# A gated-attention block on one core: the first pair placed later, one operation moved to ScalarE, GpSimd's transfers in parts

## The chip, the core and the metric

The kernel runs on one NeuronCore of a Trainium2 chip. Five engines work beside each other, each with its own queue in order: TensorE (PE: matrix products; its weight loads are listed as PEld), VectorE (DVE), ScalarE (ACT), GpSimd (POOL) and SyncE (SP, which here issues most loads). Sixteen DMA engines move data. The metric is the device time of one execution, in microseconds (us). Less is better.

## The reference

One decoder block over 256 tokens of width 2048, in float32. After a root-mean-square norm, one projection w_in gives q, k, v, an output gate, a low-rank decay, three streams for a short convolution and two merge gates:

```python
gk = einsum('bsr,rk->bsk', gk_low, w_gk_up) + b_gk_up
log_g = log_sigmoid(gk) / 16
# chunks of 64 tokens, 4 heads; bcum = cumsum(log_g) within a chunk
q_dec, k_dec = q * dk**-0.5 * exp(bcum), k * exp(-bcum)
o = tril(q_dec @ k_dec.T) @ v + q_dec @ state      # state carried from chunk to chunk
y_a = rmsnorm(o, gla_norm_w) * silu(g_out)
y_b = gate_b * (u[t-2]*w[0] + u[t-1]*w[1] + u[t]*w[2])   # u = gate_c * xc
h = x + (sigmoid(merge_a) * y_a + sigmoid(merge_b) * y_b) @ w_out
h = h + (silu(rmsnorm(h) @ w_gate) * (rmsnorm(h) @ w_up)) @ w_down
out = rmsnorm(h)
```

The hidden width is 5632. Nearly all the arithmetic lies in the products with w_in, w_out, w_gate_up and w_down.

## The kernel before

**Precision.** Each fp32 product is made of three products of a 32-bit format with fewer bits: every operand is split into a high part (`hi`) and a rest (`lo`), and `mm3` (L358) adds hi·lo, lo·hi and hi·hi. So each weight piece of 128 x 1024 is loaded by SyncE (`raw`), cast by ScalarE (`high`, L246 to 249) and subtracted by VectorE (`low`, L251 to 254) before TensorE can use it.

**Pieces.** A group of 512 output columns comes in eight pieces ("eights", `eights`, L398): 12 matmuls of 512 columns for a piece. Some groups go in pairs (`PAIRS_IN`, L76) by a scheme with seven block products in place of eight (`sevens`, L423): 28 pieces of 6 matmuls, where 16 of the pieces are sums of weight blocks that VectorE adds first (`sum_of`, L256; L272 and L277). A sevens piece gives TensorE half the work of an eights piece and VectorE more. So eights pieces are dealt in between the sevens pieces: `DEAL` (L81) says after each of a pair's 28 pieces how many eights pieces follow, and `PLACE` (L77) how many stand ahead of the pair. The order in w_in is: k0 and q0 in eights (16 pieces), the eights pieces of v0 by `PLACE`, then the pairs k2 with q2, v2 with v3, gc0 with xc0 and so on, each with its eights in between. Then come the w_out groups and the hidden layer, which are dealt in the same way.

**Order.** All is issued in one program order. When a piece is taken (`take`, L348), the piece five places later is fetched and cast, and the one four places later is subtracted. The buffers (six raw, six hi, five lo) tie how far each engine can run ahead. After each piece a counter, the tick, goes up by one (L330), and work hung on that tick is issued: `later(n, f)` and `at(tick, f)`. The framework may move an instruction within its engine's queue, save where `pin` keeps it in program order. The constants at the end of the file (L1306 on) give the ticks.

**The decay tables**, ticks 11 to 27. `x_rstd` (L669) gives the norm's factor; `spread_rstd` (L675) turns it into a row by a matmul, `split_low` (L719) splits the low-rank part, and `decay_logits` (L727) makes the logits z in PSUM and reads them twice: ScalarE takes |z|, VectorE min(z, 0). ScalarE then does a sigmoid and a logarithm of the whole tile, VectorE adds (`log_decay`, L750), sums along each chunk with eight scans (`sum_decay`, L754), and makes differences (`tables_within`, L776). ScalarE takes exponentials. `tables_across` (L787) has four operations on GpSimd and three exponentials on ScalarE. `decayed` (L707) transposes k and q and multiplies them by the tables; `scores` and `attend` follow.

**Convolution.** `conv` (L970) takes u of a gc pair, copies it to u1 and u2 shifted by one and two tokens with GpSimd's DMAs (`move`, L974), and multiplies and adds in five pinned steps on VectorE (`step`, L981). The taps are loaded by GpSimd (`load_taps`, L966). `merge` (L995) joins the branches. In the w_out stage `read_h` (L1120) loads the residual x in four parts, the first from SyncE's queue, the others from GpSimd's.

Of the kernel before, what the change touches and what calls it, by code (L numbers as in the profile page):

```python
# [43 lines left out]
def plan():  # L44
# [32 lines left out]
PLACE = (4, 0, 4, 0, 0, 0, 0)  # L77
# [4 lines left out]
    "k2": "00100 10010 01110 01010 00101000",  # L82
    "v2": "10100 11110 01200 00210 10000100",
    "gc0": "10011 00201 21111 22121 00210001",
    "gc1": "01110 11111 01002 00210 00010001",
    "gc2": "10110 12211 11202 11110 01000111",
    "gc3": "01111 01121 01001 11201 00111010",
    "g3": "30100 00100 00210 01201 00000000",
# [102 lines left out]
def block_kernel(ctx, tc, x, xt, cols_in, gkw_in, gku_in, gnw, conv_w, finw, w_in, w_out, w_gu, w_dn, out):  # L191
# [54 lines left out]
    def high(raw, piece, a=0, b=None):  # L246
        hi, n = piece[0], piece[2]
        ks = slice(a, b or n)
        nc.scalar.copy(hi[:, ks, :], raw[:, ks, :])  # L249
# [377 lines left out]
    eps = const.tile([P, 1], F32, name="eps")  # L627
    mask = gpool.tile([P, NT, P], I8, name="mask")
# [46 lines left out]
    def spread_rstd():  # L675

        rb_ps = aux([P, T], "rb_ps")
        for t in range(NT):
            spread = gpool.tile([P, P], F32, tag="sch", name="spread", bufs=2)
            nc.vector.tensor_scalar(out=spread, in0=ones, scalar1=r1[:, t:t + 1], scalar2=None, op0=ALU.mult)  # L680
            nc.tensor.matmul(rb_ps[:, t * P:(t + 1) * P], lhsT=spread, rhs=ident, start=True, stop=True)
        nc.vector.tensor_copy(rb, rb_ps)
# [14 lines left out]
    later(12, spread_rstd)  # L697
# [29 lines left out]
    def decay_logits(m0):  # L727
# [7 lines left out]
        for j in range(2):  # L735
            m = m0 + j
            nc.scalar.activation(za[:, m, :], zp[:, j, :], AF.Abs, bias=bgk[:, m:m + 1])
            nc.vector.tensor_scalar(out=zm[:, m, :], in0=zp[:, j, :], scalar1=bgk[:, m:m + 1], scalar2=0.0,
                                    op0=ALU.add, op1=ALU.min)
# [10 lines left out]
    def log_decay():  # L750
        nc.scalar.activation(za, za, AF.Ln)
        nc.vector.tensor_tensor(out=zm, in0=zm, in1=za, op=ALU.add)
# [50 lines left out]
    at(13, split_low)  # L803
    for i in range(4):
        at(14 + i // 2, lambda i=i: decay_logits(2 * i))
    at(17, lambda: nc.scalar.activation(za, za, AF.Sigmoid))
    at(19, log_decay)
    at(20, lambda: sum_decay(0))
    at(21, lambda: sum_decay(4))
    at(22, tables_within)  # L810
    at(23, lambda: exponential(eq, inv))
    at(25, tables_across)
# [132 lines left out]
    for n, (what, t) in enumerate((("k", 0), ("k", 1), ("q", 0), ("q", 1))):  # L945
        at(DECAY_AT + n, lambda what=what, t=t: decayed(what, 0, t, rows[f"{what}0"][:, t, :]))
# [19 lines left out]
    def load_taps(i):  # L966
        taps[i] = ew.tile([P, 3, 512], F32, tag="taps", name="taps")
        nc.gpsimd.dma_start(taps[i], conv_w[:, :, i * 512:(i + 1) * 512].to_broadcast([P, 3, 512]))

    def conv(i):  # L970
# [3 lines left out]
        def move(d):  # L974
            v = moved[d] = ew.tile([P, NT, 512], F32, tag=f"u{d}", name=f"u{d}")
            nc.gpsimd.memset(v[0:d, 0, :], 0.0)
            nc.gpsimd.dma_start(v[d:112 + d, :, :], u[0:112, :, :])
            nc.gpsimd.dma_start(v[112 + d:128, :, :], u[112:128 - d, :, :])
            nc.gpsimd.dma_start(v[0:d, 1, :], u[128 - d:128, 0, :])
# [10 lines left out]
        for d in (1, 2):  # L990
            later(MOVE_AT[d - 1], lambda d=d: move(d))
# [128 lines left out]
    def read_h():  # L1120
# [4 lines left out]
        h = dpool.tile([P, NT, D], F32, name="h")  # L1125
        for j in range(4):
            (nc.gpsimd if j else nc.sync).dma_start(h[:, :, j * 512:(j + 1) * 512], xv[:, :, j * 512:(j + 1) * 512])

    later(7, read_h)
# [243 lines left out]
```

## Time and profile before

| | |
|---|---|
| median of three runs | 1499.3 us (1497.88 to 1499.5) |
| the profiled execution's own time | 1503.38 us |
| its span, first to last instruction | 1501.5 us |
| TensorE busy | 1479.3 us, 99% of the span |
| VectorE busy | 1355.4 us, 90% |
| ScalarE busy | 908.6 us, 61% |
| GpSimd busy | 39.1 us, 3% |
| moved by DMA | 371.12 MB, 247 GB/s in the mean |
| TensorE's granted clock, mean | 0.996 of full speed |

How to read the rows. A timeline row has the start in us, the duration in us, engine, line of the kernel, operation, output and inputs, sizes and how many were merged (x8). In brackets is the idle time of that engine just before, and what ended it. A wait row says which engine and line waited for what: us in total, how often, and the longest. A window row has the stretch, its length, the busy time (and number of instructions) of PE, PEld, DVE, ACT and POOL, the granted clock, the busy share of the DMA engines and GB/s. A row of DMA issues ends with their number, KB of each and the median us from issue to landing. A row of the chain of waits has start, us, engine, output and line.

### The profile page before, as it was taken

The page shows a single profiled execution, that of the slowest core. Times are in us where ns is not written, and L with a number is a line of the kernel's source. Part 1 is how long each engine was busy: PE and PEld are TensorE (multiplying, and loading weights), DVE is VectorE, ACT ScalarE, POOL GpSimd, SP SyncE. Part 2 cuts the span into 40 slices and gives each one's busy share as a digit, 9 for nine tenths or more (in the row PEclk, how much of TensorE's full clock was granted, in tenths as well). Part 3 has the DMA queues.
Part 4 walks back from the last instruction along what each step waited for, and adds up shares of the span by engine and source line. Part 5 has one row for each costly group of instructions (what it writes and reads, how often), then busy time and mean ns, then how long its engine had stood idle before and what let it go on. Part 6 is the DMA issues. An engine that isn't in the chain of part 4 may idle for free.

```text
span 1501.5 us, 18621 instructions
## 1 busy us (share of the span) xinstructions
PE 1479.3 (99%) x6640; PEld 1217.7 (81%) x6640; DVE 1355.4 (90%) x1352; ACT 908.6 (61%) x1035; POOL 39.1 (3%) x59
## 2 busy tenths in 40 slices
PE   9989999999999999999999999999999999999998
PEld 7868888888888887878888888888888778888887
DVE  8889998878999989899888988989999999989975
ACT  8856666655455665557656755656555656555553
POOL 0030000000000000000000000000000000000000
PEclk9999999999999999999999999999999999999999
DMA  9547677777788877778866777777766877676782
GB/s 350 190 156 263 240 264 219 266 263 251 248 262 270 290 244 235 272 236 296 289 210 199 253 250 243 248 260 232 266 236 212 280 259 273 229 267 227 247 308 81
DMA packets 103581, 371.12 MB, mean 247 GB/s; under 512 B 11876, under 2 KB 12004, under 8 KB 103360
## 3 DMA queue, kind: packets, MB, share of 16 engines
q1 hardware_dynamic: 100112, 359.31, 69.8%
q0 software_dynamic: 2800, 8.89, 2.5%
q10 hardware_dynamic: 576, 1.72, 0.3%
q8 instruction: 52, 0.85, 0.2%
q14 instruction: 41, 0.34, 0.1%
HBM read 363.61 MB, written 2.10 MB: 244 GB/s over the span
## 4 chain that ended last, share of the span: by engine, by line
PE 91%; DMA 3%; DVE 3%; issue 1%; POOL 1%; ACT 1%; DVEq 0%; SPq 0%; ACTq 0%
PE fg L360 8%; PE fg L361 8%; PE fg L362 8%; PE dn L360 5%; PE dn L361 5%; PE dn L362 5%; PE gc L360 3%; PE gc L362 3%; PE gc L361 3%; PE mb L360 2%; PE wo L360 2%; PE mb L361 2%; PE mb L362 2%; PE wo L362 2%; PE wo L361 2%; PE g L360 2%
## 5 line engine op out<-in xcount | busy, mean ns | idle before, releaser
L249 ACT CAST hi<-raw 128x1024 fp32r<-128x1024 f32 (+1 forms) x674 | 692.1, 1049 | 482.1 <-DVE raw L277 202.8
L254 DVE TENSOR_TENSOR lo<-raw,hi 128x1024 fp32r<-128x1024 f32 (+1 forms) x674 | 805.7, 1216 | 84.7 <-ACT hi L249 36.5
L360 PE MATMUL dn<-lo,acth 128*128 128x512 f32 (+1 forms) x368 | 140.6, 383 | 1.1 <-DVE lo L254 1.1
L361 PE MATMUL dn<-hi,actl 128*128 128x512 f32 (+1 forms) x368 | 139.9, 380 | 0.0
L362 PE MATMUL dn<-hi,acth 128*128 128x512 f32 (+1 forms) x368 | 139.9, 380 | 0.0
L362 PE MATMUL fg<-hi,hh 128*128 128x512 f32 x288 | 112.5, 390 | 0.0
L360 PE MATMUL fg<-lo,hh 128*128 128x512 f32 x288 | 112.2, 390 | 0.0
L361 PE MATMUL fg<-hi,hl 128*128 128x512 f32 x288 | 112.2, 390 | 0.0
L360 PE MATMUL fg<-lo,sh 128*128 128x512 f32 x256 | 101.2, 395 | 0.0
L362 PE MATMUL fg<-hi,sh 128*128 128x512 f32 x256 | 99.9, 390 | 0.0
L361 PE MATMUL fg<-hi,sl 128*128 128x512 f32 x256 | 99.9, 390 | 0.0
L360 PEld LDWEIGHTS dn<-lo,acth 128*128 128x128 f32 x368 | 69.2, 188 | 16.2 <-DVE lo L254 2.9
L277 DVE TENSOR_TENSOR raw<-raw 128x1024 f32<-128x1024 f32 x60 | 73.1, 1219 | 10.1 <-DMA raw<-in_w_in_dram 7.3
L277 DVE TENSOR_TENSOR raw<-x,raw 128x1024 f32<-128x1024 f32 x60 | 73.1, 1218 | 9.5 <-DMA raw<-in_w_in_dram 8.6
L362 PEld LDWEIGHTS dn<-hi,acth 128*128 128x128 f32 x368 | 69.2, 188 | 13.2
L361 PEld LDWEIGHTS dn<-hi,actl 128*128 128x128 f32 x368 | 69.2, 188 | 12.8
L254 DVE TENSOR_TENSOR lo<-y,hi 128x1024 fp32r<-128x1024 f32 x60 | 73.1, 1218 | 3.1 <-PE fu L360 0.9
L272 DVE TENSOR_TENSOR raw<-y,x 128x1024 f32<-128x1024 f32 x60 | 73.1, 1218 | 2.4 <-DMA x<-in_w_in_dram 2.2
L277 DVE TENSOR_TENSOR raw<-raw,y 128x1024 f32<-128x1024 f32 x60 | 73.1, 1218 | 0.4
L249 ACT CAST hi<-y 128x1024 fp32r<-128x1024 f32 x60 | 63.0, 1050 | 11.3 <-PE gb L362 2.1
L361 PEld LDWEIGHTS fg<-hi,hl 128*128 128x128 f32 x288 | 54.1, 188 | 11.3 <-DVE hl L603 0.2
L360 PEld LDWEIGHTS fg<-lo,hh 128*128 128x128 f32 x288 | 54.1, 188 | 11.3
(305 smaller groups left out, 2863.8 us busy)
## 6 DMA issues: line engine op xcount, KB each, us to landing
raw<-in_w_in_dram SPq DMA_DIRECT2D x254, 512.0 KB, 4.9
raw<-in_w_gu_dram SPq DMA_DIRECT2D x176, 512.0 KB, 4.8
raw<-in_w_dn_dram SPq DMA_DIRECT2D x88, 512.0 KB, 4.5
y<-in_w_gu_dram SPq DMA_DIRECT2D x32, 512.0 KB, 5.4
x<-in_w_gu_dram SPq DMA_DIRECT2D x32, 512.0 KB, 3.8
raw<-in_w_out_dram SPq DMA_DIRECT2D x32, 512.0 KB, 4.6
y<-in_w_in_dram SPq DMA_DIRECT2D x28, 512.0 KB, 5.4
x<-in_w_in_dram SPq DMA_DIRECT2D x28, 512.0 KB, 4.6
```

Source lines behind the costliest of these rows:

```text
L249: nc.scalar.copy(hi[:, ks, :], raw[:, ks, :])
L254: nc.vector.tensor_tensor(out=lo[:, ks, :], in0=raw[:, ks, :], in1=hi[:, ks, :].bitcast(F32), op=ALU.subtract)
L272: nc.vector.tensor_tensor(out=raw, in0=y, in1=held["x"], op=ALU.add)
L277: nc.vector.tensor_tensor(out=raw, in0=x, in1=other, op=ALU.add)
L360: nc.tensor.matmul(ps, lhsT=sh, rhs=ml, start=first, stop=False, skip_group_check=onto)
L361: nc.tensor.matmul(ps, lhsT=sl, rhs=mh, start=False, stop=False, skip_group_check=onto)
L362: nc.tensor.matmul(ps, lhsT=sh, rhs=mh, start=False, stop=last, skip_group_check=onto)
```

## The change

- `PLACE` puts eight eights pieces (all of v0) ahead of the first pair in place of four, and the later deals give up four: the numbers of eights pieces within k2, v2, gc0, gc1, gc2, gc3, g3 go from 10, 14, 24, 16, 24, 20, 12 to 11, 13, 20, 16, 24, 20, 12, at other places.
- min(z, 0) on VectorE becomes Relu(-z) on ScalarE, with a negated bias made once; `log_decay` subtracts it.
- The spread of the row of factors and its matmul are parted, three ticks between; the decay chain's ticks move by one, the across tables by three.
- The decay products are issued in the order k1, q0, k0, q1, at ticks of their own.
- GpSimd's copies of u go in two halves and a remainder for each shift, the taps in three parts, h in four parts that all go from GpSimd's queue. Each part waits for the ScalarE cast issued last before it (`paced`).
- The ticks of scores, attention, convolution steps and transposes are set anew.

The diff, its core:

```diff
-PLACE = (4, 0, 4, 0, 0, 0, 0)
+PLACE = (8, 0, 4, 0, 0, 0, 0)
-    "k2": "00100 10010 01110 01010 00101000",
-    "v2": "10100 11110 01200 00210 10000100",
-    "gc0": "10011 00201 21111 22121 00210001",
-    "gc1": "01110 11111 01002 00210 00010001",
-    "gc2": "10110 12211 11202 11110 01000111",
-    "gc3": "01111 01121 01001 11201 00111010",
-    "g3": "30100 00100 00210 01201 00000000",
+    "k2": "00101 00110 02000 10120 00001000",
+    "v2": "10100 11100 01200 00210 10000100",
+    "gc0": "10001 11101 01111 12021 00210001",
+    "gc1": "10200 11110 10201 00210 00010001",
+    "gc2": "10110 11211 01402 11110 01000111",
+    "gc3": "00111 01221 00001 03201 00111010",
+    "g3": "30000 00200 00210 01200 00000100",
...
-        nc.scalar.copy(hi[:, ks, :], raw[:, ks, :])
+        held["cast"] = nc.scalar.copy(hi[:, ks, :], raw[:, ks, :])
+
+    def paced(ins):
+
+        tc.add_manual_dep(
+            ins.ins, held["cast"].ins.name,
+            mybir.DependencyInfo(mybir.DependencyClass.Sync, mybir.DependencyReason.DATA), reason="paced")
...
+        nc.scalar.activation(nbgk, bgk, AF.Copy, scale=-1.0)
...
-    later(12, spread_rstd)
+    for t in range(NT):
+        later(11, lambda t=t: spread_rstd(t))
+    later(14, rows_rstd)
...
-            nc.vector.tensor_scalar(out=zm[:, m, :], in0=zp[:, j, :], scalar1=bgk[:, m:m + 1], scalar2=0.0,
-                                    op0=ALU.add, op1=ALU.min)
+            nc.scalar.activation(zm[:, m, :], zp[:, j, :], AF.Relu, scale=-1.0, bias=nbgk[:, m:m + 1])
...
-        nc.vector.tensor_tensor(out=zm, in0=zm, in1=za, op=ALU.add)
+        nc.vector.tensor_tensor(out=zm, in0=za, in1=zm, op=ALU.subtract)
...
-    at(13, split_low)
+    at(14, split_low)
     for i in range(4):
-        at(14 + i // 2, lambda i=i: decay_logits(2 * i))
-    at(17, lambda: nc.scalar.activation(za, za, AF.Sigmoid))
-    at(19, log_decay)
-    at(20, lambda: sum_decay(0))
-    at(21, lambda: sum_decay(4))
-    at(22, tables_within)
-    at(23, lambda: exponential(eq, inv))
-    at(25, tables_across)
+        at(15 + i // 2, lambda i=i: decay_logits(2 * i))
+    for n, fn in enumerate((lambda: nc.scalar.activation(za, za, AF.Sigmoid), log_decay, lambda: sum_decay(0), lambda: sum_decay(4),
+                            tables_within, lambda: exponential(eq, inv), tables_across)):
+        at(TABLES_AT[n], fn)
...
-    for n, (what, t) in enumerate((("k", 0), ("k", 1), ("q", 0), ("q", 1))):
-        at(DECAY_AT + n, lambda what=what, t=t: decayed(what, 0, t, rows[f"{what}0"][:, t, :]))
+    for n, (what, t) in enumerate((("k", 1), ("q", 0), ("k", 0), ("q", 1))):
+        at(DECAY_AT[n], lambda what=what, t=t: decayed(what, 0, t, rows[f"{what}0"][:, t, :]))
...
-        nc.gpsimd.dma_start(taps[i], conv_w[:, :, i * 512:(i + 1) * 512].to_broadcast([P, 3, 512]))
+
+        def part(j):
+            paced(nc.gpsimd.dma_start(
+                taps[i][:, j:j + 1, :], conv_w[:, j:j + 1, i * 512:(i + 1) * 512].to_broadcast([P, 1, 512])))
+
+        for n, j in enumerate((1, 0, 2)):
+            later(TAP_AT[n], lambda j=j: part(j))
...
-        def move(d):
-            v = moved[d] = ew.tile([P, NT, 512], F32, tag=f"u{d}", name=f"u{d}")
-            nc.gpsimd.memset(v[0:d, 0, :], 0.0)
-            nc.gpsimd.dma_start(v[d:112 + d, :, :], u[0:112, :, :])
-            nc.gpsimd.dma_start(v[112 + d:128, :, :], u[112:128 - d, :, :])
-            nc.gpsimd.dma_start(v[0:d, 1, :], u[128 - d:128, 0, :])
+        def move(d, half):
+            if not half:
+                moved[d] = ew.tile([P, NT, 512], F32, tag=f"u{d}", name=f"u{d}")
+                nc.gpsimd.memset(moved[d][0:d, 0, :], 0.0)
+            v = moved[d]
+            a, b = ((0, 64), (64, 112))[half]
+            paced(nc.gpsimd.dma_start(v[a + d:b + d, :, :], u[a:b, :, :]))
+            if half:
+                nc.gpsimd.dma_start(v[112 + d:128, :, :], u[112:128 - d, :, :])
+                nc.gpsimd.dma_start(v[0:d, 1, :], u[128 - d:128, 0, :])
...
-        for d in (1, 2):
-            later(MOVE_AT[d - 1], lambda d=d: move(d))
+        for n in range(4):
+            later(MOVE_AT[n], lambda n=n: move(1 + n // 2, n % 2))
...
+        def part(j):
+            paced(nc.gpsimd.dma_start(h[:, :, j * 512:(j + 1) * 512], xv[:, :, j * 512:(j + 1) * 512]))
+
         for j in range(4):
-            (nc.gpsimd if j else nc.sync).dma_start(h[:, :, j * 512:(j + 1) * 512], xv[:, :, j * 512:(j + 1) * 512])
-
-    later(7, read_h)
+            later(READ_AT[j], lambda j=j: part(j))
+
+    later(6, read_h)
...
-TURN_AT = (4, 2, 15, 2)
-CONV_AT = (15, 17, 14, 12)
-CONV_STEP = (3, 1, 2, 4)
-MOVE_AT = (0, 4)
+TURN_AT = (7, 3, 12, 2)
+CONV_AT = (15, 15, 15, 12)
+CONV_STEP = (3, 4, 2, 4)
+MOVE_AT = (1, 3, 5, 10)
+READ_AT = (0, 4, 8, 12)
+TAP_AT = (0, 2, 7)
 TAPS_AT = 1
-DECAY_AT = 27
-SCORES_AT = (32, 37)
+DECAY_AT = (28, 26, 30, 30)
+TABLES_AT = (18, 20, 21, 22, 23, 24, 28)
+SCORES_AT = (35, 33)
 ROWS_AT = 2
-ATTEND_AT = (3, 6, 9)
-X_AT = (6, 12, 10, 13)
+ATTEND_AT = (3, 9, 9)
+X_AT = (6, 12, 11, 13)
```

More of the change, by code (lines that the diff above doesn't have):

```diff
@@ L627, in block_kernel @@
     eps = const.tile([P, 1], F32, name="eps")
+    nbgk = const.tile([P, NM], F32, name="nbgk")
     mask = gpool.tile([P, NT, P], I8, name="mask")
@@ L673, in x_rstd, with spread_rstd, rows_rstd @@
         nc.vector.tensor_scalar(out=r1q, in0=r1, scalar1=DK ** -0.5, scalar2=None, op0=ALU.mult)
-    def spread_rstd():
+    spread = {}
+    def spread_rstd(t):
+        spread[t] = gpool.tile([P, P], F32, tag="sch", name="spread", bufs=2)
+        nc.vector.tensor_scalar(out=spread[t], in0=ones, scalar1=r1[:, t:t + 1], scalar2=None, op0=ALU.mult)
+    def rows_rstd():
         rb_ps = aux([P, T], "rb_ps")
         for t in range(NT):
-            spread = gpool.tile([P, P], F32, tag="sch", name="spread", bufs=2)
-            nc.vector.tensor_scalar(out=spread, in0=ones, scalar1=r1[:, t:t + 1], scalar2=None, op0=ALU.mult)
-            nc.tensor.matmul(rb_ps[:, t * P:(t + 1) * P], lhsT=spread, rhs=ident, start=True, stop=True)
+            nc.tensor.matmul(rb_ps[:, t * P:(t + 1) * P], lhsT=spread[t], rhs=ident, start=True, stop=True)
         nc.vector.tensor_copy(rb, rb_ps)
@@ L801, in at @@
         later(tick - count["tick"], fn)
-    at(13, split_low)
+    at(14, split_low)
     for i in range(4):
-        at(14 + i // 2, lambda i=i: decay_logits(2 * i))
-    at(17, lambda: nc.scalar.activation(za, za, AF.Sigmoid))
-    at(19, log_decay)
-    at(20, lambda: sum_decay(0))
-    at(21, lambda: sum_decay(4))
-    at(22, tables_within)
-    at(23, lambda: exponential(eq, inv))
-    at(25, tables_across)
+        at(15 + i // 2, lambda i=i: decay_logits(2 * i))
+    assert ATTEND_AT[2] >= max(ATTEND_AT) and 16 < TABLES_AT[0] and list(TABLES_AT) == sorted(set(TABLES_AT)) and max(X_AT) < 15
+    assert min(DECAY_AT[:2]) > TABLES_AT[5] and min(DECAY_AT[2:]) > TABLES_AT[6] and min(SCORES_AT) > max(DECAY_AT)
+    for n, fn in enumerate((lambda: nc.scalar.activation(za, za, AF.Sigmoid), log_decay, lambda: sum_decay(0), lambda: sum_decay(4),
+                            tables_within, lambda: exponential(eq, inv), tables_across)):
+        at(TABLES_AT[n], fn)
     xsums = (sT.tile([P, 4, 4, 2, P], F32R, tag="sh", name="sh"), sT.tile([P, 4, 4, 2, P], F32R, tag="sl", name="sl"))
     def x_blocks(q):
+        assert ("x", q) in written
         work = omain.tile([P, 4, 2, P], F32, tag="m0", name="m0")
```

## The prediction

> **What bounds the kernel now.** I read the page's engine shares first, then what TensorE waited for, then the timeline and windows of each place where it waited.
>
> ```profile
> span 1501.5 us, 18621 instructions
> PE 1479.3 (99%) x6640; PEld 1217.7 (81%) x6640; DVE 1355.4 (90%) x1352; ACT 908.6 (61%) x1035; POOL 39.1 (3%) x59
> L249 ACT CAST hi<-raw 128x1024 fp32r<-128x1024 f32 (+1 forms) x674 | 692.1, 1049 | 482.1 <-DVE raw L277 202.8
> L254 DVE TENSOR_TENSOR lo<-raw,hi 128x1024 fp32r<-128x1024 f32 (+1 forms) x674 | 805.7, 1216 | 84.7 <-ACT hi L249 36.5
> ```
>
> TensorE is idle for 1501.5 - 1479.3 = 22.2 us; no multiplication is removed, so the change can only win back idle time and time at a lowered clock. Every weight piece costs ScalarE one cast (1.05 us) and VectorE one subtraction (1.22 us; about 1.13 us from start to start in a row).
>
> TensorE's waits over the whole run, and those between 60 and 110 us:
>
> ```profile
> PE k L360 <- DVE lo L254: 4.9, 4, 1.9
> PE turned L711 <- DVE exk L717: 2.2, 1, 2.2
> PE trb L611 <- DVE ml L614: 1.9, 1, 1.9
> PE gc L360 <- DVE lo L254: 1.8, 1, 1.8
> ```
>
> So there are three places. The first two rows are the first pair (k2, q2) and lose 7.1 us. The windows show a lowered clock behind two of the places:
>
> ```profile
> 90.00:100.00 10.00, 6.60 (x21) 5.23 (x22) 7.94 (x9) 6.73 (x9) 0.67 (x1) 0.66 0.52 174
> 125.00:175.00 50.00, 50.00 (x240) 41.33 (x239) 49.09 (x54) 34.24 (x41) 0.31 (x1) 1.00 0.77 267
> 300.00:350.00 50.00, 50.00 (x223) 41.39 (x222) 39.57 (x36) 27.67 (x28) 0.00 (x0) 1.00 0.76 243
> 590.00:595.00 5.00, 4.78 (x14) 3.79 (x15) 5.00 (x6) 2.98 (x4) 0.00 (x0) 0.66 0.76 220
> ```
>
> The third column is TensorE's busy time, then weight load, VectorE, ScalarE, GpSimd, and the granted clock. Matmuls started every 0.23 us at 68.69 and every 0.43 us after the stall (chain of waits, below), until about 99.3: 5.3 us at half speed, 2.65 us lost. In 590 to 595 the clock of 0.66 loses 1.7 us beside the 1.8 us of idle time before it. Together: first pair 9.75 us, the place near 590 us 3.5, the place near 651 us 1.9.
>
> Why the first pair waits, in order of time (critical chain, then timeline):
>
> ```profile
> 57.79 0.23 PE v L360
> 68.69 0.23 PE k L360
> 94.83 0.43 PE k L361
> 53.31 0.83 ACT L737 ACTIVATE za<-zp,cols 128x256 f32<-128x256 f32 x2
> 53.81 0.88 DVE L738 TENSOR_SCALAR zm<-zp,cols 128x256 f32<-128x256 f32 x2 [0.51 <-ACT za L737]
> 67.47 1.92 ACT L751 ACTIVATE za<-za 128x2048 f32<-128x2048 f32 x1
> 72.99 4.76 DVE L759 TENSOR_TENSOR_SCAN bc<-restart,zm 128x256 f32<-128x256 f32 x8
> 77.84 8.81 POOL L791 TENSOR_TENSOR exk<-bc 128x512 f32<-128x512 f32 x1 [25.73 <-DVE bc L759]
> 84.53 1.22 DVE L277 TENSOR_TENSOR raw<-raw,y 128x1024 f32<-128x1024 f32 x1
> 86.33 1.40 DVE L254 TENSOR_TENSOR lo<-raw,hi 128x1024 fp32r<-128x1024 f32 x1 [0.58 <-ACT hi L249]
> 88.60 1.05 POOL L792 TENSOR_TENSOR exk<-exk,bc 128x512 f32<-128x512 f32 x1
> 89.69 1.06 ACT L796 ACTIVATE exk<-exk 128x1024 f32<-128x1024 f32 x1 [3.39 <-POOL exk L792]
> 91.69 1.98 ACT L249 CAST hi<-raw 128x1024 fp32r<-128x1024 f32 x2
> 92.75 1.23 DVE L254 TENSOR_TENSOR lo<-raw,hi 128x1024 fp32r<-128x1024 f32 x1 [1.29 <-ACT hi L249]
> ```
>
> The pair starts at 68.69 and the scans end at 72.99 + 4.76 = 77.75. GpSimd's first subtraction then takes 8.81 us where a like one takes 1.05; it ends at 86.65, 0.9 us after VectorE's unbroken run ended (84.53 + 1.22). ScalarE stands at the exponential of its result, with casts behind it in the same queue, so the subtraction that TensorE needs ends only at 93.98. From end of scans to restart: 16.2 us.
>
> **The change, part by part.**
>
> *Four pieces more ahead of the pair.* An eights piece is 12 matmuls of 0.227 us, 2.72 us; the four before the pair took 68.69 - 57.79 = 10.9. With eight, the pair starts at 57.79 + 21.8 = 79.6.
>
> *The minimum goes to ScalarE.* Eight Relu replace eight VectorE operations (4 x 0.88 = 3.5 us). The nearest row is Abs on the same operands, 0.83 for two, so 3.3 us more on ScalarE, ahead of the logarithm; ScalarE was busy almost unbroken there, so I charge it in full. Bounds: 0 if casts behind it would have waited anyway; 3.3 otherwise. No table load stands between the Abs rows and the casts; I charge none for Relu. The small negated-bias operation early on costs 0 to 0.3 us; I take 0, since only the decay logits 40 us later read it.
> The Trainium skill's ScalarE: Activation LUTs, Rules for kernel authors, puts relu and min on VectorE, because VectorE is faster per element. The trace has 0.42 against 0.44 us for this fp32 shape out of PSUM, so the rule's margin is not there; by either, the sum is the same.
>
> *Ticks.* The logarithm moves behind one more cast (1.05 us), and the decay chain starts a tick later, which costs from 0 (casts fill the time) to 2.7 us; I take 0.8. The logarithm, ended at 69.39, then ends at 69.39 + 3.3 + 1.05 + 0.8 = 74.5. From there to the end of the scans took 8.36 us; the new end is 82.9, with bounds of 81.8 (one VectorE operation less in between) and 84.8. Against the pair's start the scans end 3.3 us in, not 9.1.
> *Where ScalarE then blocks.* The new exponential of the across tables stands at tick 28, after the cast of the pair's ninth piece; the tenth waits. By the new deal (00101 00110) the nine are seven sevens (1.36 us) and two eights: 15.0 us, with two transposed blocks 0.9, so TensorE arrives at 79.6 + 15.9 = 95.5. If the chain of 16.2 us holds, TensorE restarts at 82.9 + 16.2 = 99.1: 3.6 us of idle time, and again 2.65 us of half clock, 6.3 against 9.75. Saved: 3.5.
> Bounds: without VectorE in GpSimd's way the chain is 8.81 - 1.05 = 7.8 shorter and nothing is lost (saved 9.75). If GpSimd gets nothing until VectorE has run dry after the ninth piece, VectorE first does about 13.3 us (the tables' 1.3, seven subtractions and three sums of 1.13, a product), then come four operations of 1.05, 2.1 of exponentials, a cast and a subtraction of 2.2: 21.8 us, restart at 104.7, 9.2 idle and 2.65 slow, 2.1 us worse than before. I take the measured chain, as the order around it is nearest to it.
> The Trainium skill's SBUF — State Buffer, Who interferes with whom, says that a VectorE operation with two SBUF inputs and a GpSimd operation that reads SBUF exclude each other for a whole instruction. The 8.81 us and the 1.40 us subtraction agree; by that rule GpSimd goes forward only in VectorE's gaps.
>
> *Waits in TensorE's queue.* Logits banks are now read by ScalarE alone, 3.4 us per tick against a tick of 2.72 us, so the second pair of logits or the second half of the first v0 piece may wait: 0 to 1.2 us, I take 0.5. The rows of rstd spread earlier and matmul later: 0. Decay products reordered: same products, 0.
>
> *Copies, taps, h in parts.* Their rows, and the two waits they may cause:
>
> ```profile
> u<-u POOLq DMA_DIRECT2D x8, 448.0 KB, 6.2
> taps<-in_conv_w_dram POOLq DMA_DIRECT2D x4, 768.0 KB, 9.0
> u<-u POOLq DMA_DIRECT2D x4, 56.0 KB, 8.1
> 574.65 0.81 POOL L968 DMA_DIRECT2D taps<-in_conv_w_dram  x1 [27.16 <-DVE u L986]
> 585.54 1.23 DVE L277 TENSOR_TENSOR raw<-raw 128x1024 f32<-128x1024 f32 x1 [3.08 <-DMA raw<-in_w_in_dram]
> 641.54 0.59 POOL L977 DMA_DIRECT2D u<-u  x1 [53.02 <-DVE u L1055]
> 651.21 1.23 DVE L277 TENSOR_TENSOR raw<-x,raw 128x1024 f32<-128x1024 f32 x1 [2.40 <-DMA raw<-in_w_in_dram]
> SPq L1127 <- PE trb L611: 2.5, 1, 2.5
> ```
>
> VectorE stood 3.08 and 2.40 us for a weight piece whose load ran beside the 768 KB of taps and beside 896 KB of copies. In parts of 256 KB and less, with casts between, each load shares the engines with a quarter as much. I count both places as gone: 1.9 + 3.5 = 5.4; bounds 0 and 5.4. The cast that each part waits for holds only GpSimd's queue, where the next copies and memsets stand; VectorE's convolution steps wait for those (below). GpSimd issues eight DMAs for six per convolution, at 0.6 us on an engine 3% busy: 0. The first part of h leaves SyncE, which stood 2.5 us for it; weight loads behind it go earlier. It may land later, but the residual has some 2.5 us: 0.
>
> *Pieces dealt anew.* Each cover piece taken from a stage takes 2.72 - 1.13 = 1.6 us of VectorE's slack. The v2 pair gives up one, in a stretch with VectorE busy 49.09 of 50 us and TensorE never idle: 0 to 1.6, I take 0.4. The gc0 pair gives up four, but there VectorE has 10 us free in 50: 0. Other stages keep their number.
>
> **Sum.** 3.5 - 0.5 + 5.4 - 0.4 = 8.0 us saved. Against the profiled execution's 1503.38 (span 1501.5) that is 1495.4; that execution lies 4.1 us over the median of 1499.3, so the median goes to 1491.3.
>
> **Rivals.**
> *The pair's stall goes altogether* (GpSimd finds gaps while ScalarE does the exponentials and VectorE waits for casts): 9.75 + 5.4 saved, less small change, 1484.5. For it: VectorE stood 0.58 us exactly there. Against it: one gap serves one operation of four.
> *GpSimd starves to the end*: -2.1 - 0.5 + 5.4 - 0.4 = 2.4 saved, 1496.9, no difference that shows. For it: 8 us of unbroken VectorE in the trace; against it, products out of PSUM leave gaps.
> *The pacing does nothing*: ScalarE's casts run up to five pieces ahead, so the awaited cast may be over when GpSimd arrives, and copies go together as before: 3.5 - 0.9 = 2.6 saved, 1496.7.
> *The copies land too late* (slower): the last part for u2 is issued ten ticks after the product, the step that reads it stands at tick 16 for the last convolution, about 11 us later; issue and landing need up to 1.2 + 8.1 = 9.3. From 2 us more on, VectorE, 90% busy, stands in its queue with every weight subtraction behind it: about 2 us and 1.7 us of lowered clock in two or three of four convolutions, some 9 us, with no gain at the two places: 3.5 - 0.9 - 9 = -6.4, 1505.7. Against it: each part is smaller than the 6.2 us transfer.
>
> **How the numbers follow.** Forecast 0.45; stall gone 0.20; starving 0.15; pacing idle 0.07; copies late 0.13. About 0.2%, 3 us, is what a measurement here can tell. Faster: 0.45 + 0.20 = 0.65; same 0.15 + 0.07 = 0.22; slower 0.13. The range goes from the stall gone (1484.5, less 1) to just past no change, 1501; the forecast's own range is 1486 to 1496.
>
> **What would show it.** Right: the pair's first matmul near 79.6; scans ending 3 to 4 us after it; GpSimd's first subtraction still several us; one wait of 2 to 5 us near 95 us; no waits of VectorE on weight loads beside taps or copies, and no clock under 1 after 110 us. Wrong: idle time of TensorE near 57 us from the logits; over 8 us idle in the first pair; VectorE's convolution steps waiting for DMA; new waits on subtractions in the v2 or gc stages.

## The result and the profile after

The changed kernel takes 1490.9 us in the median of 14 runs (1485.67 to 1498.72); the kernel before, run beside it, 1499.8 (1497.88 to 1501.14). The ratio is 0.9949 with an interval of 0.9938 to 0.9959. The medians lie 8.9 us apart; the prediction had 8.0 (1491.3 from 1499.3).

The profiled execution of the changed kernel was the fastest of its 14 (1485.67), that of before (1503.38) lay 3.6 us above the median of before. So the spans of the two profiles differ by 17.5 us where the medians differ by 8.9: a profile says where time went, the medians say how much. One run of before among the experiments, 2117.98 us at a mean granted clock of 0.654, was a slow one and stays out of the ratios.

The page after: its span, then the engines.

```profile
span 1484.0 us, 18658 instructions
PE 1471.3 (99%) x6640; PEld 1213.7 (82%) x6640; DVE 1353.3 (91%) x1344; ACT 914.6 (62%) x1046; POOL 43.8 (3%) x76
```

TensorE is now idle for 1484.0 - 1471.3 = 12.7 us, against 22.2. What TensorE waited for between 52 and 112 us, the stretch of the first pair:

```profile
PE v L366 <- DVE vl L910: 1.3, 1, 1.3
PE turned L725 <- DVE eq L731: 1.0, 1, 1.0
PE v L366 <- DVE lo L260: 0.5, 1, 0.5
```

These 2.8 us stand where 7.1 stood; the waits on the pair's subtractions (k, `lo`, 4.9 us) are gone. The windows of the same kernel, with the columns as before (busy time of PE, PEld, DVE, ACT, POOL, granted clock, DMA share, GB/s):

```profile
78.00:90.00 12.00, 9.71 (x43) 7.18 (x41) 12.00 (x16) 9.49 (x11) 8.91 (x4) 1.00 0.28 74
90.00:100.00 10.00, 9.90 (x48) 7.86 (x49) 10.00 (x12) 4.60 (x6) 0.37 (x1) 1.00 0.28 86
...
125.00:175.00 50.00, 50.00 (x241) 41.52 (x240) 49.50 (x55) 35.63 (x48) 0.31 (x1) 1.00 0.73 244
...
590.00:595.00 5.00, 5.00 (x24) 4.14 (x23) 3.88 (x4) 2.11 (x2) 0.00 (x0) 1.00 1.03 405
```

The waits of 1.3 and 1.0 us (TensorE goes on at 85.18 and 90.10) and the one of 0.5 near 102 leave the clock at 1.00; the stretch from 90 to 100 has 48 matmuls where it had 21. The stretch near 590 has 24 where it had 14.

For a comparison stage by stage I take two landmarks: the first matmul of the gc0 pair and the first of w_out. They are the "first start" in the rows of the tiles (minimum, median, maximum of the duration in ns; first and last start in us). Before, then after:

```profile
L360 PE MATMUL gc<-lo,xh x96: 389/389/628, 249.4 to 632.1; 128*128 128x512 f32 x96
L360 PE MATMUL wo<-lo,mh x128: 388/389/500, 712.4 to 822.3; 128*128 128x512 f32 x128
```

```profile
L366 PE MATMUL gc<-lo,xh x96: 389/389/481, 253.1 to 618.9; 128*128 128x512 f32 x96
L366 PE MATMUL wo<-lo,mh x128: 388/389/497, 696.9 to 807.2; 128*128 128x512 f32 x128
```

By the new deals four eights pieces more (10.9 us by the prediction's figure) lie ahead of gc0 and four fewer behind it. At equal work the changed kernel reaches gc0 after 253.1 - 10.9 = 242.2 us, and takes 696.9 - 253.1 + 10.9 = 454.7 from there to w_out. The same for the experiments told below, all in us, from each kernel's one profile:

| kernel | start to gc0 | gc0 to w_out | w_out to end |
|---|---|---|---|
| before | 249.4 | 463.0 | 789.1 |
| after | 242.2 | 454.7 | 787.1 |
| after, once more (e1_again) | 242.8 | 456.3 | 788.6 |
| after, transfers whole (e2_whole_transfers) | 242.6 | 464.6 | 790.1 |
| after, parts without waits (e4_parts_unpaced) | 242.8 | 463.3 | 788.7 |
| after, taps whole (e5_whole_taps) | 242.7 | 467.0 | 788.1 |
| after, taps whole but late (e9_late_taps) | 243.8 | 460.3 | 786.8 |
| before, with transfers in parts (e3_only_parts) | 248.1 | 455.6 | 790.2 |
| before, without GpSimd in the tables (e7_before_no_pool) | 244.8 | 461.3 | 787.7 |
| after, old deals (e8_old_deal) | 251.6 | 457.6 | 789.0 |

The profile of e3_only_parts shares everything up to gc0 with that of before and gets there 1.3 us sooner, so some 1 us of the 7.2 saved ahead of gc0 is that one profile's own. The middle stage varies more: e10, e11 and e12 (below) do there what the changed kernel does and take 459.0, 456.3 and 458.5 us, against its 454.7.

### The profile page after: what moved, and what is told of

It is laid out like the page before. It is cut to its first block, busy times and chain, and to the rows that moved or that the text cites. A ratio compares the mean times of both kernels' runs of the same rounds, so it can differ in the third digit from the quotient of the medians.

```text
span 1484.0 us, 18658 instructions
## 1 busy us (share of the span) xinstructions
PE 1471.3 (99%) x6640; PEld 1213.7 (82%) x6640; DVE 1353.3 (91%) x1344; ACT 914.6 (62%) x1046; POOL 43.8 (3%) x76
## 4 chain that ended last, share of the span: by engine, by line
PE 97%; DVE 2%; ACT 0%; DMA 0%; issue 0%; DVEq 0%; ACTq 0%
PE fg L367 8%; PE fg L366 8%; PE fg L368 8%; PE dn L366 5%; PE dn L367 5%; PE dn L368 5%; PE gc L368 3%; PE gc L366 3%; PE gc L367 3%; PE g L366 2%; PE g L368 2%; PE g L367 2%; PE wo L366 2%; PE gb L368 2%; PE gb L366 2%; PE gb L367 2%
```

## The experiments

Twelve experiments were run; each time is a median beside that of the kernel before on the same chip (1498.84, 1500.23 and 1498.76 us in the three groups, e1 to e4, e5 to e8, e9 to e12).

### e1_again: the changed kernel once more

Edit: none.

> The changed kernel once more, to see what varies: its runs lie between 1485.67 and 1498.72 us, those of the kernel before between 1497.88 and 1501.14. Theory A (what is left are short waits that now and then grow into a lowered clock): a median near 1491, and a profile of a longer run has a lowered clock at one or two places that the first profile of it (span 1484.0) does not have. Rival B (the whole kernel runs a little slower in some runs, for instance by slower loads everywhere): the longer profile has the same places, with the difference spread over all stages.

Measured: 1491.18 us (1489.4 to 1492.59), ratio 0.9951 [0.9938, 0.9963]. The gain repeats. Its profile is 3.7 us longer than the first one of the same kernel. No stretch of 5 us has a lowered clock while matmuls run, so theory A's sign did not come. There are short waits that the first profile lacks (of the first row it has one of 0.9 us), by this view of TensorE's waits:

```profile
PE k L366 <- DVE lo L260: 2.0, 2, 1.3
...
PE ma L366 <- DVE o L1052: 0.8, 1, 0.8
```

By the landmarks the 3.7 us are spread over all three stages (0.6, 1.6 and 1.5). So executions of one kernel differ by short waits at several places. What makes them come and go I can't tell from these runs.

### e2_whole_transfers: the new order, the transfers as before

Edit to the changed kernel:

```diff
...
+        nc.gpsimd.dma_start(taps[i], conv_w[:, :, i * 512:(i + 1) * 512].to_broadcast([P, 3, 512]))
...
+            nc.gpsimd.dma_start(v[d:112 + d, :, :], u[0:112, :, :])
...
+            (nc.gpsimd if j else nc.sync).dma_start(h[:, :, j * 512:(j + 1) * 512], xv[:, :, j * 512:(j + 1) * 512])
...
-MOVE_AT = (1, 3, 5, 10)
+MOVE_AT = (0, 4)
```

> The changed kernel with the copies of u, the taps and h as before: whole, from the old queues, at the old ticks, no wait for casts. Theory A (two parts that add, the transfers worth 5.4 us as predicted): 1490.9 + 5.4, about 1496, with TensorE waiting again beside a copy or the taps in the later gc pairs, and a clock under 1 there. Rival B (all of the gain is in the first pair, the transfers give nothing): 1491, and no new wait.

Measured: 1500.12 us (1497.15 to 1503.49), ratio 1.0006 [0.9996, 1.0017]. Nothing is left of the gain, though the first pair is as good as in the changed kernel (window of 70 to 110 us of this kernel: 37.17 us busy at a clock of 1.00). Theory A's waits came, but the loss lies beyond both theories (1496 and 1491). The time is given back behind gc0: near 500 us, where before has no wait, with a clock of 0.66 behind it, and near 588, close to the place near 590 of before, but with a longer wait:

```profile
PE ma L366 <- DVE o L1042: 3.5, 1, 3.5
PE mb L366 <- DVE lo L260: 2.9, 2, 2.7
```

The wait of 2.7 us leaves the clock at 1.00. So the two halves of the change don't add: in the new order whole transfers cost more than in the old one.

### e3_only_parts: the old order, the transfers in parts

Edit to the kernel before:

```diff
-        nc.scalar.copy(hi[:, ks, :], raw[:, ks, :])
+        held["cast"] = nc.scalar.copy(hi[:, ks, :], raw[:, ks, :])
...
+            paced(nc.gpsimd.dma_start(
+                taps[i][:, j:j + 1, :], conv_w[:, j:j + 1, i * 512:(i + 1) * 512].to_broadcast([P, 1, 512])))
...
+            paced(nc.gpsimd.dma_start(v[a + d:b + d, :, :], u[a:b, :, :]))
...
+            paced(nc.gpsimd.dma_start(h[:, :, j * 512:(j + 1) * 512], xv[:, :, j * 512:(j + 1) * 512]))
...
-MOVE_AT = (0, 4)
+MOVE_AT = (1, 3, 5, 10)
+READ_AT = (0, 4, 8, 12)
+TAP_AT = (0, 2, 7)
```

> The kernel before with only the transfers in parts, each waiting for a cast. Theory A: 1499.8 - 5.4, about 1494.4, the waits near 586 and 651 us gone, the first pair's wait of 7 us still there. Rival B: 1499.8.

Measured: 1495.64 us (1494.36 to 1499.41), ratio 0.9983 [0.9973, 0.9992]: 3.2 us by the medians, where 5.4 were expected. The first pair's stall stays whole (waits of 4.9 us on subtractions and 2.2 on the table), the places near 590 and 651 us are clear. But h comes late here, which costs some of it (a row of TensorE's waits, then one of VectorE's):

```profile
PE tr L603 <- DVE h L1128: 1.9, 2, 1.3
```

```profile
DVE h L1128 <- DMA h<-in_x_dram: 3.3, 1, 3.3
```

### e4_parts_unpaced: the parts without their waits

Edit to the changed kernel:

```diff
     def paced(ins):
-        tc.add_manual_dep(
-            ins.ins, held["cast"].ins.name,
-            mybir.DependencyInfo(mybir.DependencyClass.Sync, mybir.DependencyReason.DATA), reason="paced")
+        return ins
```

> The changed kernel with its transfers in parts, but without the waits for casts. Theory A (the waits spread the parts in time and are needed): the parts of one copy go together, 1493 to 1496, with a wait of VectorE on a weight load beside a copy. Rival C (smaller transfers are enough, the waits do nothing): 1491.

Measured: 1496.3 us (1494.0 to 1498.18), ratio 0.9988 [0.9979, 0.9998]; beside the changed kernel in the same group (1491.18) the waits of all the parts together are worth 5.1 us. Without them the parts leave back to back. First all the copies of one u, from 433.05 to 437.2: ScalarE's cast at 446.46 has then stood 5.79 us for a weight load, TensorE stands 2.5 us until 448.82, and the clock is 0.83 from 445 to 455. In this kernel GpSimd's timeline, then a row of TensorE's waits:

```profile
433.05 1.07 POOL L996 DMA_DIRECT2D u<-u  x2 [32.92 <-DVE u L1075]
```

```profile
PE mb L364 <- DVE lo L258: 4.0, 2, 2.5
```

Then the three parts of the taps. GpSimd's timeline of this kernel:

```profile
476.68 1.66 POOL L980 DMA_DIRECT2D taps<-in_conv_w_dram  x3 [39.46 <-DVE u L1006]
```

and that of the changed kernel, where a cast releases each:

```profile
475.00 0.57 POOL L982 DMA_DIRECT2D taps<-in_conv_w_dram  x1 [28.32 <-ACT hi L249]
...
478.55 0.54 POOL L982 DMA_DIRECT2D taps<-in_conv_w_dram  x1 [2.99 <-ACT hi L249]
...
487.15 0.54 POOL L982 DMA_DIRECT2D taps<-in_conv_w_dram  x1 [5.87 <-ACT hi L249]
```

Behind these taps ScalarE stands 4.37 us and TensorE 1.3 near 502; behind the next ones TensorE stands 1.6 near 586. So cutting without waiting is not enough: more than half of the gain is lost, and the longest single wait stands behind the copies, not the taps.

### e5_whole_taps: only the taps whole, at the moment of the first part

Edit to the changed kernel:

```diff
...
-        for n, j in enumerate((1, 0, 2)):
-            later(TAP_AT[n], lambda j=j: part(j))
+        nc.gpsimd.dma_start(taps[i], conv_w[:, :, i * 512:(i + 1) * 512].to_broadcast([P, 3, 512]))
```

> The changed kernel with only the taps as before: one load of 768 KB, no wait for a cast. With all three kinds of transfers whole, the profile had the stalls at 490 and 592 us, each a dozen us after a whole taps load (473.94, 574.37). Theory A (of the transfers the taps are what stalls TensorE): nearly all of the 9 us comes back, 1497 to 1500, with a wait of ScalarE on a weight load of 4 to 5 us right after the taps load. Rival B (the copies are what stalls): 1491 to 1493.

Measured: 1499.77 us (1496.13 to 1503.1), ratio 1.0 [0.9991, 1.001]. One transfer, issued four times, takes the whole gain away. How, in the timeline of this kernel (GpSimd, SyncE's queue, ScalarE, VectorE):

```profile
474.92 0.79 POOL L980 DMA_DIRECT2D taps<-in_conv_w_dram  x1 [24.30 <-DVE u L1002]
...
476.92 0.33 SPq L243 DMA_DIRECT2D y<-in_w_in_dram  x1
477.34 3.88 SPq L314 DMA_DIRECT2D raw<-in_w_in_dram  x4
...
486.05 1.05 ACT L249 CAST hi<-raw 128x1024 fp32r<-128x1024 f32 x1 [4.43 <-DMA raw<-in_w_in_dram]
487.13 1.23 DVE L260 TENSOR_TENSOR lo<-raw,hi 128x1024 fp32r<-128x1024 f32 x1 [3.12 <-ACT hi L249]
```

The taps go out just ahead of five weight loads that SyncE issues in a batch. ScalarE then stands 4.43 us for a weight load, and VectorE 3.12 us for ScalarE's cast. TensorE lives on its lead until about 497. The windows of the same kernel:

```profile
475.00:480.00 5.00, 5.00 (x24) 4.14 (x23) 4.94 (x5) 1.05 (x1) 0.70 (x1) 1.00 0.78 133
...
495.00:500.00 5.00, 2.52 (x12) 1.75 (x10) 5.00 (x6) 3.55 (x5) 0.00 (x0) 1.00 0.55 175
500.00:505.00 5.00, 4.63 (x13) 3.67 (x14) 5.00 (x6) 3.46 (x5) 0.00 (x0) 0.66 1.03 371
...
585.00:590.00 5.00, 1.48 (x6) 1.24 (x7) 2.77 (x3) 3.84 (x5) 0.29 (x1) 0.97 0.90 366
590.00:595.00 5.00, 5.00 (x17) 3.96 (x16) 5.00 (x5) 2.42 (x4) 0.22 (x1) 0.69 0.40 124
```

From 475 to 480 the DMA engines are busy for 0.78 of the time but move only 133 GB/s; the changed kernel has 270 GB/s at a busy share of 0.80 in that stretch. The same happens a stage later (taps at 575.15). The idle times of 2.8 and 3.7 us and the lowered clock behind them (0.34 and 0.31 of 5 us) make some 10 us, against 12.3 more between gc0 and w_out than in the changed kernel. Not all of it is the taps': the wait near 498 also stands, shorter, in profiles with the taps in parts (0.8 us in e1_again, 2.4 in e10_min_on_vector, 2.0 in e12_h_as_before).

### e6_whole_copies: only the copies of u whole

Edit to the changed kernel:

```diff
...
+            nc.gpsimd.dma_start(v[d:112 + d, :, :], u[0:112, :, :])
...
-MOVE_AT = (1, 3, 5, 10)
+MOVE_AT = (0, 4)
```

> The changed kernel with only the copies of u as before: whole, at ticks 0 and 4, no wait for a cast. Theory A (taps): 1491 to 1493. Rival B (copies): 1497 to 1500, with VectorE waiting for a weight load beside a copy.

Measured: 1490.86 us (1486.71 to 1492.99), ratio 0.9946 [0.9932, 0.9959]: the changed kernel's time. In the new order the copies in parts, each behind a cast, win nothing over whole copies at the old ticks.

### e7_before_no_pool: the kernel before, the across tables' four operations on VectorE

Edit to the kernel before:

```diff
-        nc.gpsimd.tensor_tensor(out=exk[:, :, 0:C], in0=last(0), in1=ch(0), op=ALU.subtract)
+        nc.vector.tensor_tensor(out=exk[:, :, 0:C], in0=last(0), in1=ch(0), op=ALU.subtract)
...
```

> The kernel before with the four operations of the across tables on VectorE, 4 x 0.65 = 2.6 us there, none on GpSimd. Theory A (the first pair waits because GpSimd's reads are shut out by VectorE, the chain is 7.8 us longer for it): the first pair's idle time of 7 us falls to 2 or 3 us and the lowered clock behind it goes, 5 to 7 us saved, 1492 to 1494. Rival B (VectorE itself is what is short there, so every operation more adds to the wait): 1499 or more.

Measured: 1494.13 us (1493.57 to 1497.99), ratio 0.9967 [0.9955, 0.9978]: 6.1 us by the medians, from an edit of four lines. ScalarE's exponential starts at 85.86 and waits for nothing, against 89.69 after 3.39 us of waiting before. The pair still loses 5.1 us, in four waits on VectorE's subtractions, where 2 or 3 were expected, but the clock holds. By the landmarks 4.6 us of the gain lie ahead of gc0. Its waits between 60 and 112 us, then a window:

```profile
PE k L360 <- DVE lo L254: 5.1, 4, 2.3
```

```profile
70.00:110.00 40.00, 34.74 (x167) 27.46 (x166) 40.00 (x48) 23.18 (x27) 0.31 (x1) 1.00 0.47 158
```

So GpSimd's delay behind VectorE set ScalarE's 3.39 us in the old order: with the four operations on VectorE that wait is gone, and with it the lowered clock.

### e8_old_deal: the changed kernel with the old deals

Edit to the changed kernel:

```diff
-PLACE = (8, 0, 4, 0, 0, 0, 0)
+PLACE = (4, 0, 4, 0, 0, 0, 0)
-    "k2": "00101 00110 02000 10120 00001000",
+    "k2": "00100 10010 01110 01010 00101000",
...
```

The deals of v2, gc0 to gc3 and g3 go back in the same way.

> The changed kernel with the old deal: four eights pieces ahead of the first pair, the old strings for the pairs in w_in; the new ticks, Relu and transfers stay. Theory A (the four pieces ahead are what clears the first pair): its stall comes back and is longer, since the chain has become later by 3 us and more: over 10 us idle time and lowered clock, 1498 to 1502. Rival B (ticks and Relu do it): 1491 to 1494.

Measured: 1499.98 us (1497.88 to 1505.1), ratio 1.0005 [0.9995, 1.0015]. Transfers in parts, new ticks and Relu without the new deals win nothing. GpSimd's first subtraction again takes long, and the stretch up to gc0 takes 2.2 us more than in the kernel before. Timeline, then a window, of this kernel:

```profile
81.66 7.68 POOL L804 TENSOR_TENSOR exk<-bc 128x512 f32<-128x512 f32 x1 [26.07 <-DMA raw<-in_w_in_dram]
...
88.35 0.68 DVE L731 TENSOR_TENSOR eq<-eq,turned 128x512 f32<-128x512 f32 x1
...
93.35 1.06 ACT L809 ACTIVATE exk<-exk 128x1024 f32<-128x1024 f32 x1 [5.53 <-POOL exk L805]
```

```profile
70.00:110.00 40.00, 33.69 (x147) 26.86 (x146) 35.35 (x39) 23.68 (x25) 12.99 (x5) 0.87 0.39 130
```

Against e3_only_parts (old deals and ticks, parts) the new ticks, the new order of the decay products and Relu together cost about 3 us here (0.2 us faster than before against 3.2): the scans end at 81.57 in place of 76.59, with no more work ahead of the pair to cover it.

### e9_late_taps: the taps whole, but late and behind a cast

Edit to the changed kernel:

```diff
...
-        for n, j in enumerate((1, 0, 2)):
-            later(TAP_AT[n], lambda j=j: part(j))
+        later(TAP_AT[2], lambda: paced(
+            nc.gpsimd.dma_start(taps[i], conv_w[:, :, i * 512:(i + 1) * 512].to_broadcast([P, 3, 512]))))
```

> The changed kernel with the taps in one load of 768 KB, waiting for a cast, at the tick of the last of the three parts (seven after the call). Theory A (the size is what stalls: while the one load runs, weight loads crawl, 133 GB/s at a busy share of 0.78 between 475 and 480 us, wherever it stands): 1497 to 1500, with a wait of ScalarE on a weight load some us after each taps load. Rival B (the moment is what stalls: the taps go out just where VectorE's convolution step leaves no lead): 1491 to 1493.

Measured: 1492.07 us (1491.24 to 1493.7), ratio 0.9955 [0.9943, 0.9967]. The same 768 KB in one load, landing after 9.0 us in the median (8.4 in e5_whole_taps), go out at 492.51 and 585.75 in place of 474.92 and 575.15, and the median is that of the changed kernel to 1 us. The window that read 0.69 in e5_whole_taps:

```profile
590.00:595.00 5.00, 5.00 (x24) 4.14 (x23) 3.91 (x4) 1.47 (x2) 0.00 (x0) 1.00 0.97 256
```

So the size alone does not stall TensorE. Theory A's sign is there all the same: behind the load at 401.83 ScalarE waits 2.52 and 3.14 us for weight loads and TensorE 1.78, behind the one at 585.75 ScalarE waits 3.89 and TensorE's lead covers it. This run changed the moment and the wait for a cast together; which of the two does it was not tried.

### e10_min_on_vector: the minimum back on VectorE

Edit to the changed kernel:

```diff
-            nc.scalar.activation(zm[:, m, :], zp[:, j, :], AF.Relu, scale=-1.0, bias=nbgk[:, m:m + 1])
+            nc.vector.tensor_scalar(out=zm[:, m, :], in0=zp[:, j, :], scalar1=bgk[:, m:m + 1], scalar2=0.0,
+                                    op0=ALU.add, op1=ALU.min)
...
-        nc.vector.tensor_tensor(out=zm, in0=za, in1=zm, op=ALU.subtract)
+        nc.vector.tensor_tensor(out=zm, in0=zm, in1=za, op=ALU.add)
```

> The changed kernel with min(z, 0) on VectorE as before, eight operations of 0.44 us there and eight of 0.36 to 0.42 less on ScalarE. Theory A (ScalarE's queue sets the end of the logarithm, as the prediction charged with 3.3 us): the scans end near 78 in place of 81.0 us and the time is the same or up to 2 us less, 1489 to 1491. Rival B (VectorE is what is short in the first pair): 1492 to 1494 and a longer wait there.

Measured: 1489.52 us (1488.33 to 1491.77), ratio 0.9937 [0.9925, 0.9949]. The logarithm starts at 68.81 in place of 70.95 and the scans end at 78.87 in place of 81.0: Relu puts the chain back by 2.1 us. For the whole time that is 1 to 2 us at most; the intervals of this kernel and the changed one overlap, so no gain is shown.

### e11_no_pool: the changed kernel, the across tables on VectorE

Edit to the changed kernel:

```diff
-        nc.gpsimd.tensor_tensor(out=exk[:, :, 0:C], in0=last(0), in1=ch(0), op=ALU.subtract)
+        nc.vector.tensor_tensor(out=exk[:, :, 0:C], in0=last(0), in1=ch(0), op=ALU.subtract)
...
```

> The changed kernel with the four operations of the across tables on VectorE. In the changed kernel ScalarE no longer waits for GpSimd (89.44, no idle time before it), while VectorE is busy without a gap from 75 to 100 us. Theory A (GpSimd's lock on VectorE's reads costs about as much as the operations themselves, 3.75 us for two subtractions in place of 2.35): no difference, 1490 to 1492. Rival B (VectorE is short there and 2.6 us more make the wait longer): 1493 to 1495.

Measured: 1491.61 us (1489.47 to 1493.7), ratio 0.9948 [0.9936, 0.996]. What was worth 6.1 us in the old order is worth nothing in the new one: GpSimd isn't in the way any more.

### e12_h_as_before: h from SyncE and GpSimd as before

Edit to the changed kernel:

```diff
-            later(READ_AT[j], lambda j=j: part(j))
+            (nc.gpsimd if j else nc.sync).dma_start(h[:, :, j * 512:(j + 1) * 512], xv[:, :, j * 512:(j + 1) * 512])
...
-    later(6, read_h)
+    later(7, read_h)
```

> The changed kernel with the residual h loaded as before: the first part from SyncE, three together from GpSimd, no wait for casts. Theory A (of the transfers only the taps count): 1490 to 1492. Rival B (the parts of h count too): 1493 or more, with a wait of TensorE's transposes on h in the w_out stage.

Measured: 1492.24 us (1489.02 to 1493.74), ratio 0.9951 [0.9938, 0.9963]. TensorE waits 0.8 us for h here, but the interval is that of the changed kernel: in the new order the parts of h win nothing that can be told.

## Why the prediction was right, and where it was not

The total was right, 8.0 us for 8.9, and in part by luck: two terms were off in opposite directions. By the landmarks the stretch up to gc0 gave 5 to 7 us, where the sum has 3.5 less the small terms of 0.9. Of the 8.9 us that leaves 2 to 4 for the transfers, where the sum has 5.4; they are worth 9 us only against a loss in the new order that the sum did not have.

**The first pair: 3.5 predicted; 5 to 7 by the landmarks up to gc0, with the small terms of that stretch in it.** By the timelines the pair's first matmul starts at 78.80 against 68.53, 10.3 us later; 10.9 were predicted. The timeline of the changed kernel shows the rest of the chain:

```profile
70.95 1.92 ACT L764 ACTIVATE za<-za 128x2048 f32<-128x2048 f32 x1
...
76.25 4.76 DVE L772 TENSOR_TENSOR_SCAN bc<-restart,zm 128x256 f32<-128x256 f32 x8
...
81.09 4.27 POOL L804 TENSOR_TENSOR exk<-bc 128x512 f32<-128x512 f32 x1 [25.78 <-DVE bc L772]
...
84.38 1.40 DVE L910 SCALAR_TENSOR_TENSOR vl<-v,r,vh 128x512 fp32r<-128x512 f32 x2
85.33 1.03 POOL L806 TENSOR_TENSOR exk<-bc 128x512 f32<-128x512 f32 x1
85.70 3.75 DVE L260 TENSOR_TENSOR lo<-raw,hi 128x1024 fp32r<-128x1024 f32 x2
86.33 2.04 POOL L805 TENSOR_TENSOR exk<-exk,bc 128x512 f32<-128x512 f32 x1
88.33 2.04 POOL L807 TENSOR_TENSOR exq<-bc 128x512 f32<-128x512 f32 x1
...
89.44 1.05 ACT L809 ACTIVATE exk<-exk 128x1024 f32<-128x1024 f32 x1
```

- "The logarithm ... ends at 69.39 + 3.3 + 1.05 + 0.8 = 74.5": it ends at 72.87, and the scans at 81.0, not 82.9. The start of the chain was charged too high; of the 3.3 for Relu, e10_min_on_vector shows 2.1.
- "If the chain of 16.2 us holds" is the step that failed: it did not hold. GpSimd's first subtraction did not take 8.81 us but 4.27, and it ends at 85.36, inside the two operations on v that start at 84.38. These read v out of PSUM. v0 is now wholly done before the pair, so this read comes just when GpSimd waits, where before only subtractions and sums stood. After it the roles change: GpSimd has the tables and VectorE's two subtractions take 3.75 us where two in a row usually take 2.35 (1.22 and 1.13). ScalarE finds the table ready at 89.44 and waits for nothing. So there is no wait near 95 us, no lowered clock, and TensorE loses 2.8 us in short waits. This is nearly the rival "the pair's stall goes altogether", chance 0.20, though not by the gap of 0.58 us that it weighed. What let it happen, "products out of PSUM leave gaps", stood as an argument against another rival, "GpSimd starves to the end". (By its own terms, 9.75 + 5.4 - 0.5 - 0.4, the rival's time is 1485.0, not 1484.5.)
- Not all of the old stall was that chain. Of the 7.1 us, TensorE waited 2.3 until 78.93 and 81.26, when VectorE had been in its scans (72.99 to 77.75) and GpSimd's first subtraction had only begun. e7_before_no_pool still has these waits (1.84 and 0.46). In the changed kernel the scans end 2.2 us after the pair's first matmul, not 9.2, and the waits are gone: the prediction's landmark (3.3 for 9.1) foresaw that. In e8_old_deal, without the four pieces ahead, a wait of 4.1 us on VectorE's subtraction stands there.
- The rule weighed there, the Trainium skill's SBUF — State Buffer, Who interferes with whom, says that a VectorE operation with at most one SBUF input, outside VectorE's 2-port modes, doesn't shut GpSimd out, one with two does. The prediction took from it that GpSimd goes forward only in VectorE's gaps, which is too narrow. The traces agree with the rule: in the nine profiles with the new deals and these operations on GpSimd, the first subtraction ends 0.97 to 0.99 us after the operations on v start, and alone such a subtraction takes 1.03 us (the row at 85.33). In e10_min_on_vector both come 2.1 us earlier. In e8_old_deal it is VectorE's product with `turned`, also out of PSUM, at 88.35: GpSimd's 7.68 us end at 89.34, 0.99 us after it starts. In the kernel before, where no such operation came first, the 8.81 us end 0.9 us after VectorE ran out of work.
- e7 and e11 agree: taking GpSimd out is worth 6.1 us in the old order and nothing in the new. That it was the operation on v that let GpSimd through is read from these timelines; no run moved that operation alone.

**The logits' wait, -0.5.** It does not show: between 56 and 78 us TensorE is busy without a break, though three of its weight loads wait 0.7 us in all for Relu's results there. The 1.3 us that TensorE waited for `vl` is another one, later, and was not foreseen.

**Deals and ticks, -0.4.** As a term by itself this can't be told from 0: from 110 to 350 us the profile after shows no idle time of TensorE, that of before 0.75 us, and e1_again's 0.7. But the deals were not small. e8_old_deal says that without them the rest wins nothing, e2_whole_transfers that without the parts they win nothing. The prediction treated order and transfers as terms that add. By the medians, against before: parts alone -3.2, new order alone +1.3 (an interval that includes no change), both together -7.7 to -8.9. The two don't add up to it; each needs the other.

**The transfers, +5.4.** Between gc0 and w_out the changed kernel's profile is 8.3 us shorter than that of before, e1_again's 6.7. But the 5.4 us were read from one profile, which lay 3.6 us above the median. e7_before_no_pool does in this stage what the kernel before does, and its profile takes 461.3 us there; the two places lose less, and the clock stays at 1.00 from 590 to 595:

```profile
PE trb L611 <- DVE ml L614: 1.6, 1, 1.6
PE gc L360 <- DVE lo L254: 1.3, 1, 1.3
```

That is 2.9 us, near the 3.2 that e3_only_parts saves. The two places named, near 590 and 651 us, are clear in the changed kernel and in e3_only_parts, as foreseen. VectorE's waits for weight pieces of w_in between 110 and 720 us, before and after:

```profile
DVE raw L277 <- DMA raw<-in_w_in_dram: 15.9, 10, 3.1
```

```profile
DVE raw L283 <- DMA raw<-in_w_in_dram: 4.4, 6, 1.5
```

They are not gone, but no longer than 1.5 us, and TensorE's lead covers them. ScalarE's waits for the same loads changed little, from 23.4 to 20.7 us in 27 waits each. After 110 us no stretch of 5 us with matmuls in it shows a clock under 1. Two steps were wrong:

- "Each load shares the engines with a quarter as much. I count both places as gone." The amount alone is not what counts. With the same 768 KB in one load the time is 1499.8 or 1492.1, as it goes out ahead of a batch of weight loads or later and behind a cast (e5_whole_taps, e9_late_taps). With all transfers cut but none held back it is 1496.3 (e4_parts_unpaced), and there TensorE's longest wait stands behind the copies. The rival "the pacing does nothing" falls with e4: the waits are worth 5.1 us.
- The place near 651 was put down to the copies. In the new order the copies may be whole at no cost (e6_whole_copies), and TensorE has no wait there. How much of the old order's loss was the copies' was not tried.

The term was also measured against the wrong thing. In the new order the taps, as they were, would have cost some 9 us more than now, in the old order all the transfers together cost about 3. Why the old order bore them better is seen in part: before issued the taps at 574.65 as well, and SyncE followed with two loads at 576.65 and 577.09 and a batch only from 580.10, where e5 has the batch at once. That this is the whole difference was not tried (old convolution ticks with whole transfers in the new deals would be the test).

**h, 0.** Right in the new order as far as can be told (e12_h_as_before), wrong in the old: there the same parts came late and TensorE lost 1.9 us on them (e3_only_parts). The "some 2.5 us" of room was not room in both.

**Copies too late (slower).** VectorE's convolution steps wait for no DMA in the changed kernel. The argument against this rival, that each part is smaller, is not what kept them in time: the parts of 256 and 192 KB land after 6.0 and 6.3 us in the median, the whole 448 KB before after 6.2.

## What to carry to other kernels

A side transfer is priced by what is issued next to it: before cutting it smaller, look for the batch in the load queue and try the whole transfer later, behind work that holds it back; here that brought back all but some 1 us of what three paced parts gave. When small GpSimd operations stand on a path, list what VectorE does in just that stretch, operation by operation, and whether its inputs are in SBUF or PSUM; a reordering that puts a read out of PSUM there can be worth as much as moving the operation (here, by the timelines). Two parts of a change that use the same lead are tried together and each alone: here each half alone won 3 us or nothing, and both 8 to 9.

## What the hardware showed that was not expected

- In the 5 us behind the issue of a load of 768 KB, which repeats three rows of DRAM over all partitions, the DMA engines are busy for 0.78 of the time and move 133 GB/s (e5_whole_taps), and ScalarE then waits 4.43 us for a weight load. With two thirds of it issued in the same stretch, 3.5 us apart, they move 270 GB/s at 0.80 (the changed kernel).
- Single waits of TensorE of 2.8 and 3.7 us were followed by stretches at a clock of 0.66 and 0.69 (e5_whole_taps), while one of 2.7 left it at 1.00 (e2_whole_transfers) and 5.1 us in four waits of at most 2.3 between 76 and 96 us left it at 1.00 too (e7_before_no_pool). The Trainium skill's TensorE: Matmul & The Clock Gate, What's actually happening, ties the clock to windows of about 3.4 us that run free of the kernel, and lowers it after an idle one. Here less idle time than a whole window was enough: in the kernel before, 1.8 us near 590 was followed by 0.66, while 1.9 us near 651 was followed by 24 matmuls in 5 us at 1.00. That the same wait does the one or the other agrees with windows that do not start with the wait; no run here shows the windows themselves.
- Sixteen ScalarE operations on logits, Abs and Relu in turn, start 0.36 us apart, and no table load stands between the two functions: eight Relu take 2.9 us of ScalarE. Two of them in the timeline of the changed kernel:

```profile
60.55 0.57 ACT L751 ACTIVATE za<-zp,cols 128x256 f32<-128x256 f32 x1
60.91 0.58 ACT L752 ACTIVATE zm<-zp,nbgk 128x256 f32<-128x256 f32 x1
```
